# Down products ahead of the transposes, quarters first in up, and other places for scatters and gathers, in the expert stage of a two-layer trunk

## The chip, the cores and the metric

The kernel runs on one core of a Trainium2 chip. The metric is device time in microseconds. Before the change the median of three runs is 1512.02 us (1510.33 to 1512.49).

## The reference

Two layers over 256 tokens of 1024 columns, in float32. Layer 0 mixes tokens (RWKV-7 heads and forgetting attention) and ends in a dense SwiGLU. Layer 1 is a Conformer convolution and then a mixture of experts, which is what the change touches:

```python
def swiglu(x, w_gate, w_up, w_down):
    return (jax.nn.silu(x @ w_gate) * (x @ w_up)) @ w_down

logits = (xt @ w_router).astype(jnp.float32)
top_v, top_i = lax.top_k(logits, TOP_K)            # 2 of 8 experts for each of 256 tokens
top_w = jax.nn.softmax(top_v, axis=-1)
gates = jnp.sum(jax.nn.one_hot(top_i, N_EXPERTS) * top_w[..., None], axis=1)
for e in range(N_EXPERTS):                         # w_gate, w_up: 1024 x 3584, w_down: 3584 x 1024
    y = y + gates[:, e:e + 1] * swiglu(xt, w_gate[e], w_up[e], w_down[e])
```

A token belongs to two experts, so an expert needs only its own rows, 64 on average. All weights of all experts are read all the same.

## The kernel before

The stages follow each other: the mix of layer 0, its dense network, the convolution, and from about 575 us on the experts.

**Order of the experts.** A router counts and sorts the experts by their number of tokens. Seven are done one after the other, called experts 0 to 6 here in the order of their turn (`turn`, the index `n` in the code). The eighth, the one with the most tokens ("the largest", `big`), has no turn of its own: its work is cut into 21 phases, and `extra` says behind which chunk of which expert a phase stands (one in expert 1, six in 2, four in 3, three in 4, one in 5, six in 6).

**Chunks.** The hidden width 3584 is cut into 7 chunks of 512. A chunk of an expert is: gate (`project`, "g"), SiLU on ACT, up (`project`, "u"), `hidden`: DVE multiplies SiLU(gate) by up (L1311), TensorE transposes the product in blocks of 128 columns (L1314), ACT copies the transposes to SBUF (L1316). The down product (`down`) of a chunk runs one chunk later, on the copy that ACT made then.

**Arms.** How many rows an expert has sets its arm, chosen when the kernel runs. In the executions here experts 0, 3 and 4 run HALF (64 rows), experts 1 and 5 MOST (96 rows), experts 2 and 6 FEW (32 rows). With 64 rows the array is split into two halves of 64 columns (L1246 for gate and up, L1331 for down), each with its own part of the output. With 32 rows it is split into four quarters (L1252, L1337). MOST does both: 64 rows in halves and then 32 in quarters. A float32 product is two passes of the array and stands as two rows in the trace. Transposes, gathers and scatters use all 128 columns.

**The largest.** Its weights are split into a high and a low part, by ACT (L197) and then DVE (L198), and each product is three passes (L1274 for gate and up, L1293 to L1295 for down). `parts` has two buffers of each half, so the splits run at most two pieces ahead of TensorE.

**Gathers and scatters.** Before an expert begins, `gather` collects its rows by products with a one-hot matrix (L1168) and transposes that matrix (L1177). After it ends, `scatter` brings its output back to the tokens (L1196), and DVE adds it up (L1197). `hooks` says behind which chunk of an expert each of them stands.

**Weights.** Each chunk of a matrix is two loads of 1 MB, issued by SP (L1230) into a ring of 12 buffers. A load can be issued when TensorE (or the split) has read what the buffer held before.

**What sets the order.** The code is written for a scheduler that moves instructions within an engine's queue where it expects a wait. So the order on an engine is near that of the code, but not the same. In what follows it is read from the built programs.

Of the kernel before, what the change touches and what calls it, by code (L numbers as in the profile page):

```python
# [27 lines left out]
FULL, MOST, HALF, FEW = "full", "most", "half", "few"  # L28
# [84 lines left out]
class Trunk:  # L113
# [1121 lines left out]
    def project(self, ex, kind, c, mode, load):  # L1235
        nc, x = self.nc, ex["x"][0]
        p = self.mpsum("gu", "gu")
        ws = [load(ex, kind, c, i) for i in range(2)]
        ks = [(ws[kk // 4][:, kk % 4], kk, kk == 0, kk == NK - 1) for kk in range(NK)]
        if mode == FULL:  # L1240
            for w, kk, st, sp in ks:
                nc.tensor.matmul(p, x[:, kk], w, start=st, stop=sp)
        if mode in (MOST, HALF):
            for w, kk, st, sp in ks:
                for h in range(2):
                    nc.tensor.matmul(p[64 * h : 64 * h + 64, :T], x[:, kk, 0:64], w[:, T * h : T * h + T],  # L1246
                                     start=st, stop=sp, tile_position=(0, 64 * h), skip_group_check=True)
        if mode in (MOST, FEW):
            o, r = (T, 64) if mode == MOST else (0, 0)
            for w, kk, st, sp in ks:  # L1250
                for q in range(4):
                    nc.tensor.matmul(p[32 * q : 32 * q + 32, o : o + P], x[:, kk, r : r + 32], w[:, P * q : P * q + P],  # L1252
                                     start=st and o == 0, stop=sp, tile_position=(0, 32 * q), skip_group_check=True)
        return p


# [83 lines left out]
    def moe(self):  # L1340
        nc, tc, a = self.nc, self.tc, self.a
        nch = NCH
# [18 lines left out]
        def load(ex, *o):  # L1361
            w = early.get(o) if ex["n"] == 0 else None
            if w is None:
                w = self.egran(wt[wi[0] % nw], ex, *o)
            wi[0] += 1
            return w
# [18 lines left out]
        exs = []  # L1385
# [9 lines left out]
        def arm(n, mode, hooks, b=0, first=True, phases=True):  # L1395
            me = exs[n]
            if b:
                me = dict(me, x=me["x"][1:])
            if not first:
                me = dict(me, n=NE)  # L1400
            h = None
            for c in range(nch + 1):
                if c < nch:
                    s = self.silu(mode, self.project(me, "g", c, mode, load))
                    last, h = h, self.hidden(mode, s, self.project(me, "u", c, mode, load))
                else:
                    last = h
                if c == nch and phases:
                    phase(n, nch - 1)
                if c > 0:  # L1410
                    ws = [load(me, "d", c - 1, i) for i in range(2)]
                    self.down(mode, last, ws, yp, c == 1, c == nch)
                if c < nch - 1 and phases:
                    phase(n, c)
                if c in hooks:
                    hooks[c]()
            self.evac(mode, yp)

        def phase(n, c):
            if c not in extra.get(n, ()):  # L1420
                return
            k = sum(len(v) for j, v in extra.items() if j < n) + extra[n].index(c)
            cc, kind = k // 3, "gud"[k % 3]
            if kind == "d":
                self.big_down(big, cc, load, ysum)
                if cc == nch - 1:
                    for b in range(2):
                        self.evac(FULL, cols(ysum[b]))
                        self.scatter(big, b)
                return  # L1430
            ps = self.big_project(big, kind, cc, load)
            for j in range(2):
                js = slice(512 * j, 512 * j + 512)
                if kind == "g":
                    nc.scalar.activation(sb[j], ps[j], AF.Silu)
                else:
                    nc.vector.tensor_tensor(sb[j], sb[j], ps[j], op=ALU.mult)
                    self.split_psum(self.bh[0][:, js], self.bh[1][:, js], sb[j])
# [15 lines left out]
        yp = [self.mpsum("yp", "y") for _ in range(2)]  # L1454
        form = value(self.cnt0[0:1, 0:1], 2)
        extra = {1: (6,), 2: (0, 1, 2, 3, 4, 6), 3: (0, 2, 4, 6), 4: (1, 3, 5), 5: (6,), 6: (0, 1, 2, 3, 4, 5)}

        def hooks(n, first, last, prev):
            h = {}
            if prev is not None:  # L1460
                h[0] = prev
            if n == 0 and first:
                h[1] = ranks
                h[2] = lambda: self.gather(big, 0)
                h[3] = lambda: self.gather(big, 1)
            if last and n < len(exs) - 1:
                h[4] = lambda: self.gather(exs[n + 1], 0)
            elif last:
                h[2] = last_rows
            return h  # L1470
# [9 lines left out]
        for s, (members, arms) in enumerate(sets):  # L1480
            w0 = wi[0]

            def go(j):
                wi[0] = w0
                for n, modes in zip(members, arms[j]):
                    prev = (lambda n=n: self.scatter(exs[n - 1], 0)) if n > 0 else None
                    if len(modes) == 2:
                        if prev is not None:
                            prev()
                        self.gather(exs[n], 1)  # L1490
                        arm(n, modes[1], hooks(n, True, False, None), 1, True, False)
                        prev = lambda n=n: self.scatter(exs[n], 1)
                    first = len(modes) == 1
                    arm(n, modes[0], hooks(n, first, True, prev), 0, first)
# [11 lines left out]
            if s + 1 < len(sets):  # L1506
                sp = [mybir.EngineType.SP]
# [120 lines left out]
```

## Time and profile before

| | |
|---|---|
| median of three runs | 1512.02 us |
| the profiled execution | 1509.74 us, its span 1508.0 us |
| TensorE busy | 1423.2 us (94% of the span) |
| VectorE, ScalarE busy | 576.1 us, 450.1 us |
| read from HBM | 422.81 MB, 281 GB/s over the span |
| most that a fortieth of the span moved | 420 GB/s |

The expert stage is some 900 us of the span. Matmuls are pipelined and their ends are modelled, so TensorE shows as busy nearly throughout it; what a piece of work costs there is read from the start of its first instruction to the start of the next piece's first, and not from its busy time.

### The profile page before, as it was taken

How to read it: one execution, taken by the hardware profiler on the slowest of the kernel's cores; microseconds unless marked ns; L12 is line 12 of the kernel's file. 1: busy time of each engine (PE TensorE's matmuls, PEld its weight loads, DVE VectorE, ACT ScalarE, POOL GpSimd, SP SyncE). 2: the span in 40 equal slices, each digit the busy share in tenths (PEclk: the TensorE clock that was granted, in tenths of full speed). 3: DMA queues.
4: the chain of work that ended last, by engine and by line, in shares of the span. 5: the costliest groups of instructions: out<-in, count | busy, mean ns of one | idle time of the engine just before them, and what ended most of it. 6: DMA issues, size and time to landing. Idle time of an engine off the chain costs nothing. (4 is left out here: it accounts for less than half of the span.)

```text
span 1508.0 us, 32342 instructions
## 1 busy us (share of the span) xinstructions
PE 1423.2 (94%) x14162; PEld 1054.7 (70%) x14162; DVE 576.1 (38%) x980; ACT 450.1 (30%) x747; POOL 37.7 (3%) x63
## 2 busy tenths in 40 slices
PE   7999999999979998999999999999999999999995
PEld 6867768999966676656556787766666755657882
DVE  3855457555587663101002433321221210023435
ACT  5433435444456742110002232211211100013231
POOL 1100010000001100000000000000000000000000
PEclk8999999999989999999999999999999999999998
DMA  7322045555642238989988999899999999898992
GB/s 257 113 86 86 29 167 164 178 191 191 178 106 85 85 130 337 418 337 418 407 308 306 406 418 411 341 420 420 419 420 419 392 377 353 304 343 339 416 417 116
DMA packets 107208, 426.23 MB, mean 283 GB/s; under 512 B 6842, under 2 KB 55994, under 8 KB 64032
## 3 DMA queue, kind: packets, MB, share of 16 engines
q1 hardware_dynamic: 105968, 420.15, 72.3%
q0 software_dynamic: 1072, 3.74, 0.7%
q8 instruction: 118, 1.93, 0.5%
q14 instruction: 50, 0.41, 0.1%
HBM read 422.81 MB, written 1.05 MB: 281 GB/s over the span
## 5 line engine op out<-in xcount | busy, mean ns | idle before, releaser
L172 DVE TENSOR_TENSOR wl<-w,wh 128x1024 fp32r<-128x1024 f32 x122 | 150.8, 1239 | 120.5 <-ACT wh L170 120.1
L170 ACT ACTIVATE wh<-w 128x1024 fp32r<-128x1024 f32 x122 | 128.7, 1058 | 155.4 <-PE gu L209 56.4
L1311 DVE TENSOR_TENSOR sl<-sl,gu 128x256 f32<-128x256 f32 (+2 forms) x49 | 20.6, 421 | 400.6 <-PE gu L1252 244.1
L1274 PE MATMUL gu<-xl,bl 128*128 128x256 f32 x448 | 125.8, 286 | 3.4 <-DVE bl L198 3.2
L1246 PE MATMUL gu<-wr,xh 128*64 128x256 f32 x1024 | 122.2, 384 | 4.0 <-ACT yh L197 2.6
L1274 PE MATMUL gu<-xl,bh 128*128 128x256 f32 x448 | 125.6, 282 | 0.0
L1274 PE MATMUL gu<-xbl,bh 128*128 128x256 f32 x448 | 125.5, 281 | 0.0
L1246 PEld LDWEIGHTS gu<-wr,xh 128*64 128x64 f32 x1024 | 77.4, 138 | 43.9 <-issue 9.2
L208 PE MATMUL gu<-xh,wh 128*128 128x256 f32 x352 | 99.9, 286 | 2.4 <-DVE nt L825 2.4
L209 PE MATMUL gu<-xl,wh 128*128 128x256 f32 x352 | 100.2, 285 | 0.0
L210 PE MATMUL gu<-xh,wl 128*128 128x256 f32 x352 | 99.8, 284 | 0.0
L1305 ACT ACTIVATE sl<-gu 128x256 f32<-128x256 f32 (+2 forms) x49 | 18.8, 384 | 252.0 <-PE gu L1252 154.3
L1246 PE MATMUL gu<-wt,xh 128*64 128x256 f32 x768 | 93.1, 383 | 0.0
L1274 PEld LDWEIGHTS gu<-xl,bh 128*128 128x128 f32 x448 | 84.6, 189 | 5.4 <-issue 5.3
L1274 PEld LDWEIGHTS gu<-xl,bl 128*128 128x128 f32 x448 | 83.3, 188 | 5.8 <-DVE bl L198 5.8
L1274 PEld LDWEIGHTS gu<-xbl,bh 128*128 128x128 f32 x448 | 84.5, 189 | 0.1
L1331 PE MATMUL yp<-wr,ht 128*64 128x512 f32 x304 | 83.1, 600 | 0.0
L1316 ACT ACTIVATE ht<-ht 128x256 f32<-128x256 f32 (+2 forms) x49 | 18.8, 384 | 206.7 <-PE ht L1314 206.6
L1246 PEld LDWEIGHTS gu<-wt,xh 128*64 128x64 f32 x768 | 55.6, 137 | 31.2 <-issue 7.1
L198 DVE TENSOR_TENSOR bl<-wr,bh 128x1024 fp32r<-128x1024 f32 x40 | 48.1, 1224 | 56.5 <-ACT bh L197 56.5
L208 PEld LDWEIGHTS gu<-xh,wh 128*128 128x128 f32 x352 | 67.3, 192 | 3.4 <-DVE nt L825 2.0
L209 PEld LDWEIGHTS gu<-xl,wh 128*128 128x128 f32 x352 | 67.7, 192 | 0.7 <-DVE xl L826 0.3
(438 smaller groups left out, 2688.5 us busy)
## 6 DMA issues: line engine op xcount, KB each, us to landing
wr<-in_wd_dram SPq DMA_DIRECT2D x58, 1024.0 KB, 12.1
wr<-in_wg_dram SPq DMA_DIRECT2D x56, 1024.0 KB, 12.9
wr<-in_wu_dram SPq DMA_DIRECT2D x52, 1024.0 KB, 13.1
wt<-in_wg_dram SPq DMA_DIRECT2D x44, 1024.0 KB, 12.0
wt<-in_wd_dram SPq DMA_DIRECT2D x40, 1024.0 KB, 13.1
wx<-in_wu_dram SPq DMA_DIRECT2D x32, 1024.0 KB, 12.2
wt<-in_wu_dram SPq DMA_DIRECT2D x28, 1024.0 KB, 11.2
wx<-in_wd_dram SPq DMA_DIRECT2D x14, 1024.0 KB, 8.8
```

The source lines that it names most:

```text
L170: self.split_act = nc.scalar.activation(wh, w[:, k : k + g], AF.Copy)
L172: self.split_ins = nc.vector.tensor_tensor(wl, w[:, k : k + g], wh.bitcast(F32), op=ALU.subtract)
L198: nc.vector.tensor_tensor(lo, src, hi.bitcast(F32), op=ALU.subtract)
L208: nc.tensor.matmul(ps, wh[:, cols], xh[:, k], start=first and k == 0, stop=False, skip_group_check=True)
L209: nc.tensor.matmul(ps, wh[:, cols], xl[:, k], start=False, stop=False, skip_group_check=True)
L210: nc.tensor.matmul(ps, wl[:, cols], xh[:, k], start=False, stop=k == NK - 1, skip_group_check=True)
L1246: nc.tensor.matmul(p[64 * h : 64 * h + 64, :T], x[:, kk, 0:64], w[:, T * h : T * h + T], start=st, stop=sp, tile_position=(0, 64 * h), ski ...
L1274: mm = lambda l, r, st, sp: nc.tensor.matmul(o, l[:, k, cols], r[:, kk], start=st, stop=sp, skip_group_check=True)
L1305: self.nc.scalar.activation(s[:, :w], gate[:, :w], AF.Silu)
L1311: self.last_mul = nc.vector.tensor_tensor(s[:, :w], s[:, :w], up[:, :w], op=ALU.mult)
L1316: nc.scalar.activation(h[:, :w], ps[:, :w], AF.Copy)
L1331: nc.tensor.matmul(y[0][64 * d : 64 * d + 64], h[:, o : o + 64], w[:, 512 * d : 512 * d + 512], start=st, stop=sp, tile_position=(0, 64 * ...
```

## The change

Three edits. In `arm`, the down product of the chunk before is written between the up projection and `hidden` (multiply, transposes, copy), where it stood behind `hidden`. In `project`, the up projection of a MOST expert does its quarters first and its halves after them. In `hooks`, a scatter goes to the first chunk of its expert that has a phase, a gather to the first such chunk from the third on, and both stand ahead of the phase of their chunk, not behind it.

```diff
--- before.py
+++ after.py
@@ -1237,20 +1237,25 @@
         p = self.mpsum("gu", "gu")
         ws = [load(ex, kind, c, i) for i in range(2)]
         ks = [(ws[kk // 4][:, kk % 4], kk, kk == 0, kk == NK - 1) for kk in range(NK)]
-        if mode == FULL:
-            for w, kk, st, sp in ks:
-                nc.tensor.matmul(p, x[:, kk], w, start=st, stop=sp)
-        if mode in (MOST, HALF):
+        def wide():
             for w, kk, st, sp in ks:
                 for h in range(2):
                     nc.tensor.matmul(p[64 * h : 64 * h + 64, :T], x[:, kk, 0:64], w[:, T * h : T * h + T],
-                                     start=st, stop=sp, tile_position=(0, 64 * h), skip_group_check=True)
-        if mode in (MOST, FEW):
+                                     start=st and not up, stop=sp, tile_position=(0, 64 * h), skip_group_check=True)
+
+        def narrow():
             o, r = (T, 64) if mode == MOST else (0, 0)
             for w, kk, st, sp in ks:
                 for q in range(4):
                     nc.tensor.matmul(p[32 * q : 32 * q + 32, o : o + P], x[:, kk, r : r + 32], w[:, P * q : P * q + P],
-                                     start=st and o == 0, stop=sp, tile_position=(0, 32 * q), skip_group_check=True)
+                                     start=st and (up or o == 0), stop=sp, tile_position=(0, 32 * q), skip_group_check=True)
+
+        up = kind == "u" and mode == MOST
+        if mode == FULL:
+            for w, kk, st, sp in ks:
+                nc.tensor.matmul(p, x[:, kk], w, start=st, stop=sp)
+        for f in {MOST: (narrow, wide) if up else (wide, narrow), HALF: (wide,), FEW: (narrow,)}.get(mode, ()):
+            f()
         return p
 
 
@@ -1398,22 +1403,21 @@
                 me = dict(me, x=me["x"][1:])
             if not first:
                 me = dict(me, n=NE)
-            h = None
             for c in range(nch + 1):
                 if c < nch:
                     s = self.silu(mode, self.project(me, "g", c, mode, load))
-                    last, h = h, self.hidden(mode, s, self.project(me, "u", c, mode, load))
-                else:
-                    last = h
-                if c == nch and phases:
+                    up = self.project(me, "u", c, mode, load)
+                elif phases:
                     phase(n, nch - 1)
                 if c > 0:
                     ws = [load(me, "d", c - 1, i) for i in range(2)]
-                    self.down(mode, last, ws, yp, c == 1, c == nch)
+                    self.down(mode, h, ws, yp, c == 1, c == nch)
+                if c < nch:
+                    h = self.hidden(mode, s, up)
+                if c in hooks:
+                    hooks[c]()
                 if c < nch - 1 and phases:
                     phase(n, c)
-                if c in hooks:
-                    hooks[c]()
             self.evac(mode, yp)
 
         def phase(n, c):
@@ -1457,14 +1461,16 @@
 
         def hooks(n, first, last, prev):
             h = {}
+            ph = extra.get(n, ()) if last else ()
             if prev is not None:
-                h[0] = prev
+                h[next((c for c in ph if c < nch - 1), 0)] = prev
             if n == 0 and first:
                 h[1] = ranks
                 h[2] = lambda: self.gather(big, 0)
                 h[3] = lambda: self.gather(big, 1)
             if last and n < len(exs) - 1:
-                h[4] = lambda: self.gather(exs[n + 1], 0)
+                at = [c for c in ph if 3 <= c < nch - 1 and c not in h]
+                h[at[0] if at else 4] = lambda: self.gather(exs[n + 1], 0)
             elif last:
                 h[2] = last_rows
             return h
```

The first place is TensorE's queue in expert 1 (MOST), from the up projection of chunk 2 on: `gu` is the projection, `yp` the down product, `ht` the transposes, `wx` and `wt` are weights. Before:

```order
L1246 MATMUL gu_7752<-wx_5515,xh_5551 64x256 x8
L1246 MATMUL gu_7752<-wx_5516,xh_5551 64x256 x8
L1252 MATMUL gu_7752<-wx_5515,xh_5551 32x128 x16
L1252 MATMUL gu_7752<-wx_5516,xh_5551 32x128 x16
L1331 MATMUL yp_5673<-wt_5517,ht_7671 64x512
L1314 MATMUL ht_7804<-cstT,sl_7750 128x128 x3
L1331 MATMUL yp_5673<-wt_5517,ht_7671 64x512 x3
L1331 MATMUL yp_5673<-wt_5518,ht_7671 64x512 x4
L1337 MATMUL yp_5674<-wt_5517,ht_7671 32x256 x8
L1337 MATMUL yp_5674<-wt_5518,ht_7671 32x256 x8
```

The same place now:

```order
L1250 MATMUL gu_7699<-wr_5530,xh_5551 32x128 x16
L1250 MATMUL gu_7699<-wr_5531,xh_5551 32x128 x16
L1250 MATMUL gu_7752<-wx_5515,xh_5551 32x128 x16
L1250 MATMUL gu_7752<-wx_5516,xh_5551 32x128 x16
L1243 MATMUL gu_7752<-wx_5515,xh_5551 64x256 x8
L1243 MATMUL gu_7752<-wx_5516,xh_5551 64x256 x8
L1336 MATMUL yp_5673<-wt_5517,ht_7697 64x512 x4
L1336 MATMUL yp_5673<-wt_5518,ht_7697 64x512 x4
L1342 MATMUL yp_5674<-wt_5517,ht_7697 32x256 x8
L1342 MATMUL yp_5674<-wt_5518,ht_7697 32x256 x8
L1319 MATMUL ht_7830<-cstT,sl_7750 128x128 x3
L1243 MATMUL gu_7836<-wt_5519,xh_5551 64x256 x8
```

The quarters of up now follow those of gate, the halves of up are followed by the halves of down, and the transposes have left the middle of the down product for its end. The chunks of expert 5 read alike, and chunks 3 and 4 of both before had a second break, with one product of the quarters between two halves of the down product.

The second place is TensorE's queue in expert 0 (HALF), the end of chunk 2, where a gather follows (`ga`, `ot`). Before:

```order
L1331 MATMUL yp_5673<-wt_5517,ht_5772 64x512
L1314 MATMUL ht_5870<-cstT,sl_5848 128x128 x2
L1331 MATMUL yp_5673<-wt_5517,ht_5772 64x512 x3
L1331 MATMUL yp_5673<-wt_5518,ht_5772 64x512 x4
L1168 MATMUL ga_5888<-oh_5885,tok_5277 128x128 x8
L1168 MATMUL ga_5899<-oh_5885,tok_5277 128x128 x8
L1177 MATMUL ot_5910<-cstT,oh_5885 128x128 x2
```

The same place now:

```order
L1336 MATMUL yp_5673<-wt_5517,ht_5780 64x512 x4
L1336 MATMUL yp_5673<-wt_5518,ht_5780 64x512 x4
L1319 MATMUL ht_5880<-cstT,sl_5848 128x128 x2
L1168 MATMUL ga_5888<-oh_5885,tok_5277 128x128 x8
L1168 MATMUL ga_5899<-oh_5885,tok_5277 128x128 x8
L1177 MATMUL ot_5910<-cstT,oh_5885 128x128 x2
```

The transposes stand behind the whole down product and ahead of the gather. In experts 0, 3 and 4 ten down products lose their break in this way: chunks 1 to 5 of expert 0 (in chunk 5 the transposes go to the middle, between two even halves), 1, 3 and 5 of expert 3, and 2 and 4 of expert 4 (chunk 6 of it too, where the down product that follows waits for the copy). Where a phase of the largest follows, the transposes stood ahead of the down product as a whole, and still do, in most places.

The third place is TensorE's queue in expert 4 (HALF), from the transposes ahead of the scatter (`sca`) of expert 3. Before, behind chunk 0:

```order
L1314 MATMUL ht_14158<-cstT,sl_14136 128x128 x2
L1196 MATMUL sca_14163<-yh,oht_5641 128x512
L1196 MATMUL sca_14163<-yl,oht_5641 128x512
L1246 MATMUL gu_14179<-wt_5517,xh_5551 64x256
L1196 MATMUL sca_14167<-yh,oht_5641 128x512
L1196 MATMUL sca_14167<-yl,oht_5641 128x512
L1246 MATMUL gu_14179<-wt_5517,xh_5551 64x256 x2
L1196 MATMUL sca_14171<-yh,oht_5641 128x512
L1196 MATMUL sca_14171<-yl,oht_5641 128x512
L1246 MATMUL gu_14179<-wt_5517,xh_5551 64x256
L1196 MATMUL sca_14175<-yh,oht_5641 128x512
L1196 MATMUL sca_14175<-yl,oht_5641 128x512
```

Now, behind chunk 1:

```order
L1319 MATMUL ht_14214<-cstT,sl_14182 128x128 x2
L1196 MATMUL sca_14219<-yh,oht_5641 128x512
L1196 MATMUL sca_14219<-yl,oht_5641 128x512
L1196 MATMUL sca_14223<-yh,oht_5641 128x512
L1336 MATMUL yp_5673<-wr_5526,ht_14161 64x512 x4
L1196 MATMUL sca_14223<-yl,oht_5641 128x512
L1196 MATMUL sca_14227<-yh,oht_5641 128x512
L1196 MATMUL sca_14227<-yl,oht_5641 128x512
L1196 MATMUL sca_14231<-yh,oht_5641 128x512
L1336 MATMUL yp_5673<-wr_5527,ht_14161 64x512 x4
L1196 MATMUL sca_14231<-yl,oht_5641 128x512
L1298 MATMUL y_14237<-bh_14239,bhh 128x512
```

The scatter was spread among the gate's halves of chunk 1, and now stands among the down product of chunk 0, directly ahead of a phase of the largest (`y`). The gather of expert 4 has moved in the same way, from behind chunk 4, which has no phase, to chunk 3, ahead of a phase. In expert 2 the gather has moved from the phase of chunk 4 to that of chunk 3. The other scatters stood ahead of the phase before, and stand there now. The order of the loads on SP is unchanged within an expert.

## Rows read from the trace of the kernel before

**Rows 1.** Windows of experts 0, 1, 3, 5: us, busy by engine, PEclk, DMA share, GB/s.

```profile
582.30:675.50 93.20, 91.94 (x677) 55.68 (x676) 13.43 (x54) 12.73 (x27) 0.00 (x0) 1.00 0.91 368
678.60:802.80 124.20, 124.12 (x1651) 74.34 (x1653) 8.55 (x17) 7.37 (x16) 0.00 (x0) 0.99 0.95 378
...
952.40:1071.50 119.10, 115.09 (x824) 79.70 (x824) 27.55 (x38) 20.95 (x32) 0.00 (x0) 0.99 1.01 415
...
1215.30:1339.60 124.30, 123.18 (x1653) 73.56 (x1655) 8.75 (x15) 8.32 (x17) 0.00 (x0) 1.00 0.89 340
```

**Rows 2.** Waits of PE in the expert stage: total us, times, longest us.

```profile
PE ht L1314 <- DVE sl L1311: 12.8, 23, 0.8
...
PE gu L1274 <- DVE bl L198: 3.2, 4, 1.2
```

**Rows 3.** Waits of ACT in the same stretch.

```profile
ACT bh L197 <- DMA wt<-in_wd_dram: 2.6, 2, 1.4
```

**Rows 4.** Timeline of PE, chunk 2 of expert 1 (start us, us, engine, line, tiles).

```profile
713.20 3.67 PE L1246 MATMUL gu<-wr,xh 128*64 128x256 f32 x32
716.80 1.95 PE L1252 MATMUL gu<-wr,xh 128*32 128x128 f32 x64
718.69 3.67 PE L1246 MATMUL gu<-wx,xh 128*64 128x256 f32 x32
...
724.18 1.07 PE L1331 MATMUL yp<-wt,ht 128*64 128x512 f32 x2
725.18 0.55 PE L1314 MATMUL ht<-cstT,sl 128*128 128x128 f32 x3
725.66 3.65 PE L1331 MATMUL yp<-wt,ht 128*64 128x512 f32 x14
729.24 1.93 PE L1337 MATMUL yp<-wt,ht 128*32 128x256 f32 x32
731.10 0.44 PE L1246 MATMUL gu<-wt,xh 128*64 128x256 f32 x2
```

**Rows 5.** Timeline of PE, end of chunk 3 of expert 1.

```profile
749.69 0.65 PE L1246 MATMUL gu<-wr,xh 128*64 128x256 f32 x4
```

**Rows 6.** Timeline of PE, chunk 3 of expert 0, up to its gather.

```profile
636.64 3.62 PE L1246 MATMUL gu<-wx,xh 128*64 128x256 f32 x32
640.09 1.02 PE L1331 MATMUL yp<-wt,ht 128*64 128x512 f32 x2
641.04 0.44 PE L1314 MATMUL ht<-cstT,sl 128*128 128x128 f32 x2
641.41 3.65 PE L1331 MATMUL yp<-wt,ht 128*64 128x512 f32 x14
644.99 0.38 PE L1168 MATMUL ga<-oh,tok 128*128 128x128 f32 x1
```

**Rows 7.** Timeline of PE, a down product of expert 3 in one piece.

```profile
1071.52 3.65 PE L1331 MATMUL yp<-wt,ht 128*64 128x512 f32 x16
1075.11 0.39 PE L1274 MATMUL gu<-xl,bh 128*128 128x256 f32 x1
```

**Rows 8.** Timeline of PE, quarters of expert 2.

```profile
929.79 1.93 PE L1252 MATMUL gu<-wt,xh 128*32 128x128 f32 x64
931.53 1.93 PE L1252 MATMUL gu<-wr,xh 128*32 128x128 f32 x64
```

**Rows 9.** Timeline of PE, chunks 1 and 2 of expert 3.

```profile
983.36 1.02 PE L1331 MATMUL yp<-wr,ht 128*64 128x512 f32 x2
...
995.82 0.44 PE L1314 MATMUL ht<-cstT,sl 128*128 128x128 f32 x2 [0.58 <-DVE sl L1311]
```

**Rows 10.** Timeline of PE behind a gather: expert 2 into a phase of the largest.

```profile
911.41 0.74 PE L1293 MATMUL y<-bh,bhh 128*128 128x512 f32 x2 [1.42 <-ACT bh L197]
912.67 0.50 PE L1294 MATMUL y<-bl,bhh 128*128 128x512 f32 x1 [0.52 <-DVE bl L198]
```

**Rows 11.** Timeline of PE behind the gather of expert 3.

```profile
1040.63 0.39 PE L1274 MATMUL gu<-xl,bl 128*128 128x256 f32 x1 [1.22 <-DVE bl L198]
```

## The prediction

> **What bounds the kernel now.** I read the windows first, one per expert. They show TensorE busy almost from end to end in each, and the DMA engines full or nearly so: share 0.91 for expert 0, 0.95 for expert 1, 1.01 for expert 3, 0.89 for expert 5 [rows 1]. Either could be the bound, so the waits decide. In the whole expert stage TensorE's longest list entry is the transposes waiting for DVE's multiply, 12.8 us in 23 waits, then the split of a weight, 3.2 us [rows 2]; no wait of TensorE for a load is among them. A load shows as the end of a wait in one place, at ACT's split, 2.6 us in two waits [rows 3]. So the stage runs at TensorE's pace, with the weights a little ahead, and the rest of the kernel before it isn't touched.
>
> Next I read TensorE's timeline, from start to start. A MOST chunk lasts from 713.20 to 731.10, 17.90 us. In it the down product in halves is torn: two passes take 1.00 us (724.18 to 725.18), the three transposes 0.48, the other fourteen 3.58 [rows 4]. The same sixteen passes in one piece take 3.59 us with the step to the next shape, 1071.52 to 1075.11 [rows 7]. So the tear costs about 1.0 us beside the transposes. Two reasons fit: the passes of the two halves run side by side in pairs, and a break after an odd product leaves a pass of each without its partner at both ends (0.50 us a pass ahead of the break, 0.22 in one piece); and TensorE stands until DVE's multiply is done.
>
> **The change part by part.** Work is neither added nor removed on any engine; it moves.
>
> *Prices.* Halves of gate, then quarters: 3.60 us; quarters, then halves: 1.89 [rows 4]. Quarters followed by quarters: 1.74 (929.79 to 931.53) [rows 8], so a change of shape costs 0.15. Halves of up followed by halves of down: 3.45 (636.64 to 640.09) [rows 6]. Quarters of down, then another shape: 1.86. Transposes: 0.48 for three [rows 4] and 0.37 for two [rows 6], each with the step to the halves, so 0.11 each and 0.15 for the step.
>
> *A MOST chunk.* New order: 3.60 + 1.74 + 1.89 + 3.45 + 3.59 + 1.86 + 0.48 = 16.61 us, 1.29 less than 17.90. The multiply on DVE now has the whole down product, 5.4 us, to be done in. Chunk 3 lasted 731.10 to 749.69, 18.59 us [rows 4, 5], as a second break by a product in quarters cost 0.69 more, and chunk 4 is ordered alike: 1.98 each. In chunks 4 and 6 a gather or a phase follows the transposes at full width, so one step of 0.15 goes too. In chunk 0 there's no down product, only two changes of shape less: 0.29. One MOST expert saves 0.29 + 3 x 1.29 + 2 x 1.98 + 1.29 + 2 x 0.15 = 9.7 us; experts 1 and 5 together 19.4. The last step, transposes behind quarters, stands nowhere in the trace of before: at best it's free, at worst it drains like the halves of 64 columns, 0.95 - 0.43 = 0.5 us [rows 6]; I take the 0.15 of the other steps.
>
> *A HALF chunk.* Before a gather: 0.95 + 0.37 + 3.58 = 4.90 us from 640.09 to 644.99 [rows 6]. Now 3.59 + two transposes 0.22 = 3.81, and the gather follows in the same shape: 1.09 saved, three times in expert 0. Without a gather the next chunk's halves fill the lone passes up, so less is to be had: from 983.36 to the end of the second up, 995.82 - 0.58, are 11.9 us [rows 9], and now 3.59 + 0.37 + 2 x 3.45 + 0.2 = 11.1: 0.8 saved, in two chunks of expert 0, three of expert 3 and one of expert 4. In chunk 4 of expert 4 4.90 become 3.96, 0.9 saved. The last chunk of expert 4 gains its break back and loses about as much waiting for ACT's copy: nothing. Sum 3.3 + 6 x 0.8 + 0.9 = 9.0 us.
>
> *Hooks ahead of a phase.* The products are the same. What changes is what stands behind them in the queues of ACT and DVE: the split of the phase's weights waits until the copies of the gather or the sums of the scatter are done. The price stands in the trace where a gather is ahead of a phase already: 1.42 + 0.52 us in expert 2 [rows 10], 1.22 in expert 3 [rows 11]. New are the gather and the scatter of expert 4: 2 x 1.22 = 2.4 us. In expert 2 the stall moves with the gather from one phase to another; the phase it leaves then has only 1.86 us of quarters as cover, where copy and split take longer, and one phase there has later transposes: 0.7 in all. Bounds for these four: nothing, if the scheduler's order hides them, to twice the price, 6 us. I take 3.1. On SP the load of the last norm's rows goes four loads earlier; the weights ahead in the ring hide it.
>
> *The stream.* Expert 3 asks for 50 loads in its turn (42 of its own, 8 for four phases); at 415 GB/s a load of 1.05 MB takes 2.53 us, so 126 us, more than the 119.10 that its window has [rows 1]. It lives on what the ring holds, and ACT's two waits for loads lie there and near the end [rows 3]. What is saved ahead of such a wait is given back: I take off one HALF chunk, 0.8. Experts 1 and 5 ask for 44 loads, 111 us; they'd last 124.2 - 9.7 = 114.5. That still fits.
>
> Sum: 19.4 + 9.0 - 3.1 - 0.8 = 24.5 us off the profiled execution's 1509.74: 1485.2. The median of the runs shown is 2.3 us above that execution, so 1487.5.
>
> **The Trainium skill on the tear.** The rows show 4.90 us for a torn down product with its transposes, and by the rows of one in one piece 3.81 to 3.96 [rows 6, 7]. "TensorEngine Tiling (Array Packing)", section "Key Properties", says that a change of the tiling mode drains TensorE, while tiles run on their own; by that alone, only the number of changes counts. That is the first rival below.
>
> **Rivals.**
>
> 1. *Only the changes of shape count.* The lone passes aren't why the torn product is slow, the modelled starts only look so. Then a MOST chunk saves three changes of 0.15, 0.45 us, chunks 3 and 4 0.69 more, chunk 0 0.29; a HALF chunk 0.15 to 0.3. That is 2 x (0.29 + 6 x 0.45 + 2 x 0.69) = 8.7, plus 2.2, less 3.1: 7.8 us, 1504. For it: the busy times of these rows are modelled. Against: a pass takes 0.50 us ahead of the break and 0.22 in one piece, on starts alone [rows 4, 7]. Chance 0.07.
>
> 2. *The stream takes it back.* Wherever the DMA share is 0.94 and more, a faster TensorE waits for weights, and only experts 0 and 5 keep what they save: 3.3 + 1.6 + 9.7 = 14.6, with the stalls of the hooks hidden in the same waits: 1497. For it: shares of 0.95 and 1.01 [rows 1]. Against: TensorE's list has no wait for a load [rows 2], and 44 loads fit in 114 us. Chance 0.12. [...]
>
> 3. *Slower: the splits of the phases come late.* ACT and DVE work in order, and the copy of the transposes stands ahead of the split. If the transposes are last ahead of a phase, copy and split have no cover any more and the stall of 1.94 us [rows 10] is paid at each of 21 phases: 41 us, less 24.5 + 3.1 saved: 13 us slower, 1525. It decides from 14 such phases on. Against: in the built order the transposes stay ahead of the down product at most phases, and in expert 1 two splits stand ahead of the copy. Chance 0.03.
>
> 4. *More than forecast.* Nothing is lost at the hooks and the transposes' last step is free: 24.5 + 3.1 + 12 x 0.15 = 29, 1483. Chance 0.08, and within the range.
>
> **How the numbers follow.** The forecast has 0.70, 1482 to 1494 for it alone. The range, 1481 to 1502, adds rivals 2 and 4 and leaves out most of 1 and 3. About 0.2%, 3 us, is what a measurement of this kernel tells from no change. Rivals 1, 2 and 4 and the forecast are all faster by more: 0.93, taking 0.04 off for a mix of 1 and 2 with dear stalls, which ends within 0.2%. Slower: 0.03.
>
> **What would show it.** In the profile after: MOST chunks of 16.6 us from gate to gate; sixteen passes of L1336 without a break, 3.4 to 3.6 us; transposes behind the quarters of down with no wait for DVE, whose 12.8 us shrink to the places ahead of phases; the gathers of expert 0 directly behind the transposes; a wait of 1 to 2 us for a split behind the gather and the scatter of expert 4. Wrong would be: TensorE waits for loads in experts 1 or 5 (rival 2), MOST chunks of 17.4 us (rival 1), or waits for splits at most phases (rival 3).

## The result, and the profile after

The changed kernel took 1493.15 us (median of four runs, 1492.38 to 1499.99) against 1511.17 us of the kernel before (four runs, 1509.52 to 1512.49): a ratio of 0.9874, 95% interval 0.9847 to 0.9901. Five more runs, later, gave 1492.96 us and 0.986, 0.9839 to 0.988. The forecast was 1487.5 within 1481 to 1502, faster: right in sign and range, and 5.7 us too far down. Of the 24.5 us that the sum had taken off, 18.0 came in the medians, and 16.3 in the span of the profiled executions (1508.0 to 1491.7).

First the windows of the changed kernel, one each for experts 1, 3 and 5 (us; busy us of TensorE, its weight loads, VectorE, ScalarE and GpSimd; TensorE's granted clock; DMA share; GB/s; to be held against [rows 1]).

```profile
680.40:795.00 114.60, 113.62 (x1642) 72.29 (x1640) 9.80 (x16) 9.26 (x17) 0.00 (x0) 1.00 0.99 402
944.60:1063.60 119.00, 113.97 (x838) 77.09 (x840) 28.79 (x39) 23.26 (x35) 0.00 (x0) 1.00 1.01 416
1208.00:1322.00 114.00, 112.55 (x1646) 73.22 (x1644) 7.02 (x11) 8.31 (x16) 0.00 (x0) 1.00 0.93 357
```

The same work of a MOST expert now lasts some 114 us and not 124, and the DMA share rose with it, from 0.95 to 0.99 in expert 1. A share of 0.99 still isn't a wait: these are TensorE's longest waits in the changed kernel's expert stage (us in total, times, longest).

```profile
PE ht L1319 <- DVE sl L1316: 12.0, 21, 0.8
PE gu L1243 <- issue: 6.9, 4, 3.2
PE gu L1279 <- DVE bl L198: 6.0, 6, 1.2
...
PE y L1299 <- DVE bl L198: 2.4, 3, 1.5
```

No wait of TensorE's products for a load is in that list, short ones included, which disposes of rival 2. Its weight loads did wait for DMA, 0.3 us at a time and 2.1 us in all in experts 1 and 5, but beside running products: every chunk there with no gather or phase near takes the same 16.61 us. The first row has hardly moved from 12.8 us in 23 waits [rows 2]; the other three stand for what the change cost. Waits for the split were 3.2 us [rows 2] and 0.8 us before, and the waits with no releaser ("issue") were these:

```profile
PE gu L1246 <- issue: 4.3, 2, 2.8
```

Now TensorE's timeline of chunk 2 of expert 1, start to start, as in [rows 4].

```profile
711.35 3.67 PE L1243 MATMUL gu<-wr,xh 128*64 128x256 f32 x32
714.95 1.95 PE L1250 MATMUL gu<-wr,xh 128*32 128x128 f32 x64
716.72 1.93 PE L1250 MATMUL gu<-wx,xh 128*32 128x128 f32 x64
718.58 3.67 PE L1243 MATMUL gu<-wx,xh 128*64 128x256 f32 x32
722.09 3.60 PE L1336 MATMUL yp<-wt,ht 128*64 128x512 f32 x16
725.62 1.93 PE L1342 MATMUL yp<-wt,ht 128*32 128x256 f32 x32
727.48 0.55 PE L1319 MATMUL ht<-cstT,sl 128*128 128x128 f32 x3
727.96 3.67 PE L1243 MATMUL gu<-wt,xh 128*64 128x256 f32 x32
```

From 711.35 to 727.96 are 16.61 us, the forecast to the second decimal, and each step within 0.06 of its term: 3.60, 1.77, 1.86, 3.51, 3.53, 1.86, 0.48. Sixteen passes of L1336 run without a break, and the transposes follow the quarters without a wait. In chunk 3 of expert 0 the gather follows the transposes directly (TensorE again, against [rows 6]):

```profile
641.86 3.60 PE L1336 MATMUL yp<-wt,ht 128*64 128x512 f32 x16
645.39 0.44 PE L1319 MATMUL ht<-cstT,sl 128*128 128x128 f32 x2
645.66 3.74 PE L1168 MATMUL ga<-oh,tok 128*128 128x128 f32 x32
```

3.80 us stand where 4.90 stood; the forecast was 3.81.

**Where the time went, term by term.** The length of each chunk is the distance between two starts of ACT's silu. It repeats to 0.05 us from one profile to the next of the same code, but for the chunks behind a branch and those in which TensorE's clock fell.

| part | forecast, us saved | in the profiles |
|---|---|---|
| chunks 1 to 6 of experts 1 and 5 | 18.8 | 9.50 + 9.37 = 18.9 |
| chunk 0 of experts 1 and 5 | 0.6 | -0.39 - 0.47 = -0.9 |
| HALF chunks of experts 0, 3, 4 | 9.0 | 4.85 + 2.50 + 0.81 + 1.19 = 9.35 |
| last chunk of expert 4 | 0 | -1.4 |
| scatter and gather of expert 4 | -2.4 | -1.56 - 1.85 = -3.4 |
| expert 2 | -0.7 | -1.7 |
| stream | -0.8 | 0 |
| rest of the stage (behind branches) | 0 | 0.7 in chunk 6 of expert 0, -0.7 elsewhere: 0 |
| ahead of the expert stage | 0 | -4.6 |

The gather's 1.85 and the last 1.19 of the HALF chunks fall in the same two chunks and are told apart by after_old_hooks, below. The sum of the stage is 20.8 us for 24.5 forecast; the stage began 4.6 us later than before, at 590.67 us and not 586.10, though no edit touches what is ahead of it.

### The profile page after: what moved, and what is told of

Its sections match the earlier page's. It is cut to its first block, busy times and chain, and to the rows that moved or that the text cites. A ratio compares the mean times of both kernels' runs of the same rounds, so it can differ in the third digit from the quotient of the medians.

```text
span 1491.7 us, 32344 instructions
## 1 busy us (share of the span) xinstructions
PE 1399.1 (94%) x14162; PEld 1050.8 (70%) x14162; DVE 575.2 (39%) x980; ACT 450.8 (30%) x747; POOL 37.8 (3%) x63
## 5 line engine op out<-in xcount | busy, mean ns | idle before, releaser
L1243 PE MATMUL gu<-wr,xh 128*64 128x256 f32 x1024 | 116.9, 381 | 6.2 <-issue 3.2
L1243 PEld LDWEIGHTS gu<-wr,xh 128*64 128x64 f32 x1024 | 72.9, 137 | 45.0 <-issue 8.3
L1321 ACT ACTIVATE ht<-ht 128x256 f32<-128x256 f32 (+2 forms) x49 | 18.8, 384 | 282.4 <-PE ht L1319 282.4
L1310 ACT ACTIVATE sl<-gu 128x256 f32<-128x256 f32 (+2 forms) x49 | 18.8, 385 | 185.9 <-PE gu L1250 110.5
L1336 PE MATMUL yp<-wr,ht 128*64 128x512 f32 x304 | 69.8, 595 | 0.5 <-ACT ht L1321 0.5
L210 PEld LDWEIGHTS gu<-xh,wl 128*128 128x128 f32 x352 | 67.0, 190 | 0.6 <-DVE wl L172 0.6
```

Source lines behind the costliest of these rows:

```text
L210: nc.tensor.matmul(ps, wl[:, cols], xh[:, k], start=False, stop=k == NK - 1, skip_group_check=True)
L1336: nc.tensor.matmul(y[0][64 * d : 64 * d + 64], h[:, o : o + 64], w[:, 512 * d : 512 * d + 512], start=st, stop=sp, tile_position=(0, 64 * ...
```

## Experiments

Eleven runs followed, eight of new kernels and three repeats. The first three do one edit of the three alone, the fourth undoes one. A MOST chunk is the best measure of all: eight times (chunks 1, 2, 3 and 5 of experts 1 and 5) it repeats with no gather, scatter or phase near. In the table, which shows expert 1, T is the transposes and the numbers are passes of the halves:

| kernel | chunk 1 | 2 | 3 | order of the down product |
|---|---|---|---|---|
| before | 17.90 | 17.90 | 18.59 | 2 passes, T, 14; in chunk 3 a stray quarter too |
| arm_only | 16.90 | 17.60 | 17.60 | 16, quarters, T; in 2 and 3 a stray quarter |
| quarters_only | 17.61 | 17.61 | 17.61 | 2, T, 14 |
| break_odd | 17.61 | 17.61 | 17.61 | 10, T, 6, then the quarters |
| break_even | 16.77 | 16.76 | 16.76 | 12, T, 4, then the quarters |
| changed | 16.61 | 16.61 | 16.61 | 16, quarters, T |

### One edit alone: down ahead of the transposes

```diff
-                    last, h = h, self.hidden(mode, s, self.project(me, "u", c, mode, load))
+                    up = self.project(me, "u", c, mode, load)
...
+                if c < nch:
+                    h = self.hidden(mode, s, up)
```

> The kernel before with one edit of the three: the down products are written ahead of the transposes; quarters stay last in up, gathers and scatters stay behind the phases. Theory A (a break inside the sixteen passes of L1331 leaves two passes without their partner, and the wait for the gating product is paid in the open): a MOST chunk goes from 17.90 us to about 16.9, and from 18.59 to 16.9 in chunks 3 and 4, HALF chunks as in the changed kernel (0.8 to 1.1 less each); about 15 us in the MOST experts, 8 to 9 in the HALF ones, less about 1.4 where the code of expert 5 is fetched after a shorter tail: 1488 to 1490. Rival B (only the changes of tile shape count; a break costs two of them, 0.3 us): a MOST chunk about 17.6, 1504 to 1506. Rival C (the gain of the whole change came from quarters first): no change, 1509 to 1512.

Measured: 1490.66 us in the profiled execution, two of four runs at 1490.5 and two at 1501.6, so a median of 1496.06; ratio 0.9898, 0.985 to 0.9945. The two pairs differ in the mean granted clock, 0.980 and 0.972; the kernel is the same. The stage took 902.7 us for 921.9. Chunk 1 came as theory A has it, 16.90, and so did the HALF chunks. Chunks 2 to 4 missed it by 0.70: this is TensorE in chunk 2.

```profile
717.27 1.94 PE L1331 MATMUL yp<-wt,ht 128*64 128x512 f32 x8
719.14 0.62 PE L1337 MATMUL yp<-wt,ht 128*32 128x256 f32 x2
719.69 1.94 PE L1331 MATMUL yp<-wt,ht 128*64 128x512 f32 x8
721.56 1.93 PE L1337 MATMUL yp<-wt,ht 128*32 128x256 f32 x30
```

The scheduler draws one quarter product, two passes, in between the halves. They take 0.55 us for 0.12 among their like, and two more changes of shape come with them. The same stray made chunk 3 of the kernel before 18.59 us long. With quarters first in up it is gone. Chunk 1 puts rivals B and C out.

### One edit alone: quarters first

```diff
-                                     start=st, stop=sp, tile_position=(0, 64 * h), skip_group_check=True)
+                                     start=st and not up, stop=sp, tile_position=(0, 64 * h), skip_group_check=True)
...
+        for f in {MOST: (narrow, wide) if up else (wide, narrow), HALF: (wide,), FEW: (narrow,)}.get(mode, ()):
```

> The kernel before with one edit of the three: in up, the quarters are written ahead of the wide products. The order dw, T, dw with its broken pair stays. Theory A: 0.29 us less in each of 14 MOST chunks (two changes of tile shape fewer), less 0.7 us in the first chunk of experts 1 and 5, where the many short instructions come before the fetch of code has caught up: 2 to 3.5 us less, 1507.5 to 1509.5. Rival C (it carries the gain): 1500 or less. Rival D (the stalls of the fetch cost more than the shapes give): 1511 to 1514.

Measured: 1507.0 us (ten runs), ratio 0.9961, 0.9943 to 0.998; the stage 916.7 us, 5.2 less. More than expected, for a reason I hadn't put down: chunks 1, 2 and 5 save their 0.29, but chunks 3 and 4 save 0.98, as the stray quarter goes with the new order. Chunk 0 saved 0.31 in expert 1 and lost 1.52 in expert 5. In chunk 2 of expert 1 the transposes stand behind the first product, as in the kernel before, and wait for nothing:

```profile
726.66 1.02 PE L1336 MATMUL yp<-wt,ht 128*64 128x512 f32 x2
727.61 0.55 PE L1319 MATMUL ht<-cstT,sl 128*128 128x128 f32 x3
728.09 3.65 PE L1336 MATMUL yp<-wt,ht 128*64 128x512 f32 x14
```

### One edit alone, and one undone: gathers and scatters

```diff
+                if c in hooks:
+                    hooks[c]()
                 if c < nch - 1 and phases:
                     phase(n, c)
-                if c in hooks:
-                    hooks[c]()
...
-                h[0] = prev
+                h[next((c for c in ph if c < nch - 1), 0)] = prev
...
+                at = [c for c in ph if 3 <= c < nch - 1 and c not in h]
+                h[at[0] if at else 4] = lambda: self.gather(exs[n + 1], 0)
```

> The kernel before with one edit of the three: gathers and scatters ahead of a phase of the largest. Theory A (the product of the phase waits for the split on VectorE and ScalarE, which now has only a gather or a scatter as cover, whose matmuls wait in turn; 1.5 us each at expert 4's scatter, expert 4's gather, expert 2's gather): 4 to 5 us longer, 1515 to 1517. The prediction's own term: 3.1 us longer, 1514. Rival E (those stalls are there whichever side the gather stands, and the changed kernel's gaps are of its shorter chunks): within 1 us of before, 1510 to 1512.

> The changed kernel with that third edit undone: gathers and scatters behind the phase, at the old chunks. Theory A: 4 to 5 us shorter than the changed kernel, 1488 to 1489.5, the gain at the chunks 1 and 2 (scatter) and 4 and 5 (gather) of expert 4 and 4 and 5 of expert 2. The prediction's term: 3.1 shorter, 1490. Rival E: as the changed kernel, 1492.5 to 1494.

Measured: hooks_only 1518.44 us (ten runs), ratio 1.0033, 1.0013 to 1.0054, the stage 926.9 us, 5.0 more than before. after_old_hooks 1487.13 us (four runs), ratio to the kernel before 0.9823, 0.9795 to 0.9852, the stage 897.2 us, 3.9 less than in the changed kernel's first profile and 2.6 less than in its shortest. So this edit slows the kernel, alone and in company; rival E is out. Chunks 0 and 1 of expert 4, which hold the scatter, by ACT's silu at the start of chunk 0 and of chunk 2, in the changed kernel:

```profile
1083.18 0.39 ACT L1310 ACTIVATE sl<-gu 128x256 f32<-128x256 f32 x1 [1.52 <-PE gu L1243]
1119.24 0.39 ACT L1310 ACTIVATE sl<-gu 128x256 f32<-128x256 f32 x1 [8.16 <-PE gu L1243]
```

and in after_old_hooks:

```profile
1080.30 0.38 ACT L1310 ACTIVATE sl<-gu 128x256 f32<-128x256 f32 x1 [1.52 <-PE gu L1243]
1114.79 0.38 ACT L1310 ACTIVATE sl<-gu 128x256 f32<-128x256 f32 x1 [8.15 <-PE gu L1243]
```

36.06 us for 34.49: the scatter costs 1.57 where it now stands. TensorE of the changed kernel shows what is late, once behind the scatter and once behind the gather (two rows, far apart):

```profile
1104.58 0.51 PE L1299 MATMUL y<-bl,bhh 128*128 128x512 f32 x1 [1.52 <-DVE bl L198]
...
1144.15 0.39 PE L1279 MATMUL gu<-xl,bl 128*128 128x256 f32 x1 [1.22 <-DVE bl L198]
```

Both wait for DVE's half of the split, as forecast; 1.52 and 1.22 us for 1.22 twice. Chunks 3 and 4 of expert 4, with the gather, lose 1.85 us against after_old_hooks.

Expert 2 didn't go as theory A has it. Its chunks 3 and 4 took 42.49 us before, 42.54 in hooks_only, 44.00 in the changed kernel, and 43.98 in after_old_hooks, which has the gather where it was. The 1.5 us is not the move's. It isn't chance either: the three profiles of the changed kernel have 43.99 to 44.05, and arm_only, best_try and tail_even8, with the gather in its old place, 43.94 to 44.07. Windows of the changed kernel around that gather (columns as above):

```profile
881.00:885.40 4.40, 2.46 (x17) 2.02 (x18) 2.63 (x3) 2.28 (x3) 0.00 (x0) 1.00 1.01 413
885.40:888.80 3.40, 3.40 (x18) 3.40 (x17) 0.42 (x1) 0.09 (x1) 0.00 (x0) 0.50 1.02 422
```

and of the same stretch in break_odd (below), which has the same order and the same two waits there:

```profile
887.80:892.20 4.40, 2.46 (x17) 2.02 (x18) 2.61 (x3) 2.27 (x3) 0.00 (x0) 1.00 1.01 415
892.20:895.60 3.40, 3.40 (x31) 3.40 (x31) 0.83 (x2) 1.06 (x1) 0.00 (x0) 1.00 1.02 422
```

TensorE was busy 2.46 of 4.40 us while it waited for the split, and then got the lower of its two clocks, 0.50 (1.2 GHz), for 3.4 us. In after_old_hooks the same befell it behind its gather, at 900.0 us. In break_odd TensorE was busy for the same 2.46 of 4.40 us, the clock stayed at 1.00, and the two chunks took 42.52 us. So a wait in this place can cost itself and 1.5 us more; why the clock falls in the one kernel and not in the other stays open.

### Why a torn down product is slow

The break of the kernel before could cost a lone pass at either side, a wait for DVE's multiply, or only the two changes of shape. These two kernels put the transposes inside the down product again, but late enough that the multiply is done.

```diff
                 for d in range(2):
+                    if mid and 2 * kb + d == 5:
+                        mid()
                     nc.tensor.matmul(y[0][64 * d : 64 * d + 64], h[:, o : o + 64], w[:, 512 * d : 512 * d + 512],
...
+                    mid = (lambda: new.append(self.hidden(mode, s, up))) if mode == MOST and c < nch else None
...
```

In break_even the 5 is a 6.

> The changed kernel, but in MOST arms the transposes are written inside the sixteen wide down passes, behind the fifth of the eight products (ten passes; 2.2 us, more than the wait for the gating product). In nothing else does it differ from break_even, where they stand behind the sixth. Theory A (the passes run in pairs, one to a column half; a break behind an odd number leaves one pass without its partner on either side, 0.85 us in all): a MOST chunk 16.61 + 0.85 + up to 0.3 for the second change of shape = 17.5 to 17.8 in all twelve chunks 1 to 6, some 10 us longer than break_even. Theory B (only the change of shape costs, or the open wait): both kernels alike, 16.6 to 16.9.

> As break_odd with the transposes behind the sixth product. Theory A: 16.6 to 16.9 in a MOST chunk (no pass loses its partner; one pair of shape changes more than the changed kernel), and the whole within 4 us of the changed kernel. Theory B: as break_odd.

Measured: break_odd 1504.93 us (three runs), ratio 0.9944, 0.9924 to 0.9964. break_even 1498.42 us (two runs, 1495.14 and 1501.71; the profiled one entered the stage 6 us later than break_odd's), ratio 0.9902, 0.9871 to 0.9934. Free of that, the stage took 912.2 and 902.1 us: 10.0 longer for the odd one, as theory A has it. TensorE in chunk 2 of expert 1, break_odd:

```profile
723.54 2.74 PE L1338 MATMUL yp<-wt,ht 128*64 128x512 f32 x10
726.21 0.55 PE L1319 MATMUL ht<-cstT,sl 128*128 128x128 f32 x3
726.69 1.93 PE L1338 MATMUL yp<-wt,ht 128*64 128x512 f32 x6
728.55 1.93 PE L1344 MATMUL yp<-wt,ht 128*32 128x256 f32 x32
```

and break_even:

```profile
729.14 2.75 PE L1338 MATMUL yp<-wt,ht 128*64 128x512 f32 x12
731.82 0.55 PE L1319 MATMUL ht<-cstT,sl 128*128 128x128 f32 x3
732.29 1.08 PE L1338 MATMUL yp<-wt,ht 128*64 128x512 f32 x4
733.30 1.93 PE L1344 MATMUL yp<-wt,ht 128*32 128x256 f32 x32
```

Ten passes take as long as twelve (2.67 and 2.68 us), and six take 1.86 us where four take 1.01. No wait stands at either. Halves and transposes are 5.01 us with the odd break and 4.16 with the even one, 0.85 us for the lone passes alone. By theory B they'd be equal. Two further breaks agree: a break behind two passes and one behind ten both give 17.61 us (quarters_only, break_odd), and in best_try, below, four passes ahead of an even break take 0.96 us, where two ahead of an odd one take 0.95 [rows 6].

### Repairs, and the tail of expert 4

```diff
-        up = kind == "u" and mode == MOST
+        up = kind == "u" and mode == MOST and c > 0
...
+                    mid = (lambda: new.append(self.hidden(mode, s, up))) if n == 4 and c == nch - 1 else None
```

with the old hooks of after_old_hooks, and `mid` called behind the second down product (best_try) or the fourth (tail_even8).

> The changed kernel with the hooks of before (as after_old_hooks), and two small repairs: in the last chunk of expert 4, which no phase follows, the transposes stand behind the second of the down products, so that TensorE's last wait comes 6 us ahead of the branch and not 3.5; and the first chunk of an expert has its quarters last again. Theory A (the code behind the branch is fetched once that last wait is over, some 7 to 8.5 us): chunk 6 of expert 4 about 20 us for 23.15, or for 21.6 where no half clock fell into it; first chunks of experts 1 and 5 as before (14.9) for 15.3 and 14.7: 1484 to 1486. Rival (the gap at the branch has its fixed length behind the last product): 1486.5 to 1488, chunk 6 of expert 4 at 21.5 or more.

> As best_try, but in the last chunk of expert 4 the transposes stand behind the fourth of the down products and not the second. Twenty-four passes of 0.22 us are left behind them in place of 28. If the code behind the branch comes 6.9 us after the hidden copy is there (the changed kernel's distance): first product behind the branch 12.9 us after the chunk's start, gap 2.1. If it comes as in best_try 9.1 us behind the transposes: 14.2 us, gap 3.4. If TensorE's instructions ahead of the branch are a queue of fixed length: gap 2.5 again, first product at 13.3. The whole within 1 us of best_try, 1482.5 to 1484.5.

Measured: best_try 1483.53 us (six runs), ratio to the kernel before 0.9816, 0.9789 to 0.9843; tail_even8 1484.34 us (four), 0.9827, 0.9799 to 0.9854. Their stages, 894.9 and 895.1 us, are 5 to 6 us shorter than the changed kernel's and the shortest measured. Chunk 0 of experts 1 and 5 took 15.12 and 14.88 us with quarters last, against 15.28 to 15.62 in three profiles of the changed kernel; over all kernels with quarters first it lay anywhere from 14.58 to 16.40. At the end of expert 4 and the start of expert 5, TensorE of the changed kernel:

```profile
1199.84 0.44 PE L1319 MATMUL ht<-cstT,sl 128*128 128x128 f32 x2
1200.75 3.65 PE L1336 MATMUL yp<-wr,ht 128*64 128x512 f32 x16 [0.47 <-ACT ht L1321]
1207.64 3.67 PE L1243 MATMUL gu<-wr,xh 128*64 128x256 f32 x32 [3.23 <-issue]
...
1212.79 1.62 PE L1250 MATMUL gu<-wr,xh 128*32 128x128 f32 x51 [0.92 <-issue]
...
1217.89 2.59 PE L1243 MATMUL gu<-wx,xh 128*64 128x256 f32 x22 [0.41 <-issue]
```

The kernel before, in the same place:

```profile
1206.86 7.08 PE L1331 MATMUL yp<-wr,ht 128*64 128x512 f32 x30
1215.38 0.87 PE L1246 MATMUL gu<-wr,xh 128*64 128x256 f32 x6 [1.44 <-issue]
...
1220.65 1.73 PE L1252 MATMUL gu<-wr,xh 128*32 128x128 f32 x53 [1.04 <-issue]
```

And best_try:

```profile
1188.43 0.44 PE L1319 MATMUL ht<-cstT,sl 128*128 128x128 f32 x2
1188.80 6.23 PE L1340 MATMUL yp<-wr,ht 128*64 128x512 f32 x28
1197.55 5.36 PE L1243 MATMUL gu<-wr,xh 128*64 128x256 f32 x32 [2.53 <-issue]
```

"issue" is time in which TensorE waited for nothing that the trace shows. Behind the branch into expert 5 it grew from 1.44 to 3.23 us. The stop in the gate's quarters, ahead of chunk 0's first silu, was there before too (1.04 us, now 0.92). What is new lies in chunk 0 itself: behind two runs of quarters TensorE stops once more, 0.41 us, in the halves of up. With quarters last no profile has that stop. Theory A said that 6.9 us pass from the last wait's end (1200.75 to 1207.64); then best_try, with 28 passes behind its last transposes, would have had a gap of 1.2 us. It had 2.53, so the theory is wrong in that form. tail_even8, with 24 passes, had 2.40: the distance of 6.9 us asks for 2.1, a queue of fixed length ahead of the branch for 2.5. That speaks for the queue, but 0.3 us and two kernels don't settle it, and the kernel before, 1.44 with 30 passes at a slower pace, wasn't resolved further. best_try still gained 2.5 us in this chunk over after_old_hooks (20.69 for 23.15): 0.5 at the transposes, 0.75 at the gap, and the rest because less of the low clock fell behind the branch, which isn't shown to be the repair's work. Against the changed kernel's three profiles (21.46 to 21.73) it gained 0.8 to 1.0 us.

### The changed kernel and the kernel before, once more

Unaltered, for the 4.6 us ahead of the stage.

> The changed kernel unaltered, for how long it takes up to the expert stage, whose code no edit touches: 590.67 us in its first profile, 586.06 to 589.22 in the five others. If that was chance of the clock in that execution: 586 to 590 now, the expert stage at 901 again, the whole 1488 to 1494. If it belongs to this kernel: 590.5 to 591.

> The changed kernel unaltered, a third profile. Its first two entered the expert stage at 590.67 and 590.96 us, seven profiles of kernels with the same code up to there at 586.06 to 597.74. If that is chance of the clock in an execution, anything from 586 to 598, with half-clock time ahead of the stage to match (34 us of it at 586, 51 at 590.8, 61 at 597.7); if it belongs to the kernel, 590.5 to 591 a third time.

> The kernel before unaltered, a second profile. If chance: the stage starts anywhere from 586 to 598 (586.10 in its first). If it belongs to the kernel: 586.0 to 586.3. Either way the chunks of the stage repeat to 0.05 us but for those behind a branch and those with a half clock in them (chunk 6 of experts 0 and 4, chunk 0 of 1, 2, 3 and 5).

Measured: after_again 1492.96 us, its stage from 590.96; after_third 1492.35 us, from 590.82; before_second 1510.42 us, from 586.76. Windows from the span's start to the stage, of the changed kernel and of the kernel before:

```profile
0.00:590.60 590.60, 551.56 (x4794) 455.08 (x4796) 350.73 (x645) 281.96 (x481) 37.83 (x63) 0.96 0.43 140
```

```profile
0.00:586.10 586.10, 547.01 (x4796) 453.31 (x4798) 351.15 (x645) 281.58 (x481) 37.70 (x63) 0.97 0.44 141
```

Same instructions, same work of DVE, another mean clock. Three profiles of the changed kernel lie within 0.3 us, so by what was written beforehand the delay would belong to it; the first profiles of the others lay anywhere from 586.06 to 597.74. But other numbers on record speak against that. The runs of this kernel go from 1489.62 to 1499.99 us, at clocks of 0.979 and 0.971, and a stage that repeats to 1.3 us can't hold that spread; so the time ahead of it most likely varies from run to run. All three profiles have a low clock of 17 us near the start (from 18.4 to 35.5 us in the first), where both profiles of the kernel before have it only 3.4 to 6.8 us at a time; but break_even, with the same code up to there, has the 17 us too. So the delay is one of the granted clock, and whether it belongs to the kernel stays open.

## Why the prediction was right, and where it was off

- *MOST chunks* (19.4 us): right, and for the first of the two reasons it gave. break_odd against break_even shows the lone passes by themselves, 0.85 us; break_even against the changed kernel shows one change of shape more, 0.16; quarters_only shows the two others, 0.29. Together they make up the 1.29. The second reason, the wait for DVE's multiply, falls: the transposes in [rows 4] have no wait beside them, break_odd with the multiply long done takes 17.61 us, and quarters_only with the transposes right behind the first product takes the same. TensorE's list of the kernel before has no such wait in experts 1 and 5; its 12.8 us lay in the other five experts, ahead of phases above all, where the order stayed. I read a total over the stage as if it stood in the chunk of the argument, and so forecast that it would shrink; it is 12.0.
- *Rival 1* (only shape changes): a change of shape does cost, 0.15 us as the rows gave it, but break_odd and break_even have the same changes and differ by 0.85 us in each chunk. The Trainium skill, "TensorEngine Tiling (Array Packing)", section "Key Properties", says that a change of the tiling mode drains TensorE. The trace agrees in that each change costs, and shows that it isn't all.
- *Rivals 3 and 4*: rival 3 needed late splits at most of 21 phases; TensorE has eleven waits for a split, for seven before. Rival 4 needed nothing lost at the hooks; they lost 3.4 us.
- *Chunk 0* (0.6 us): the wrong sign, -0.9. The step "only two changes of shape less" overlooked that quarters are 64 short instructions, and that with two runs of them behind a branch TensorE stops in the halves of up, 0.38 to 0.68 us in experts 1 and 5 of all three profiles. Where quarters are first and no such stop shows (expert 1 of quarters_only, expert 5 of break_even, break_odd and after_old_hooks), the chunk took 14.58 to 14.81 us, at best the 0.3 less that was forecast. That it runs out of instructions there is argued from this and not shown. With quarters last again best_try has 14.88 to 15.12.
- *HALF chunks* (9.0 us): right, 9.35 came. The term "loses about as much waiting for ACT's copy: nothing" for the last chunk of expert 4 failed: 0.47 us of that wait and 1.8 us more at the branch, less some 0.9 that the lone passes and a shorter stop in the quarters gave back: -1.4.
- *Hooks* (-3.1 us): the mechanism right in expert 4 and its size too small, 3.4 for 2.4 us. The two waits shown are 2.7 of it, and the scatter's own wait for DVE's sum is 0.4; the rest isn't resolved. In expert 2 the 0.7 for the moved stall was nothing (0.05 in hooks_only), and 1.5 us of low clock came in its place, in all three profiles.
- *The stream* (-0.8 us): nothing. Every HALF chunk of expert 3 kept its 0.83 us at a DMA share of 1.01. Rival 2's sign was products waiting for loads in experts 1 or 5, and there are none.
- *Ahead of the stage*: 4.6 us that no term held. It is the largest single piece of the 8.2 us between the forecast and the profiled execution.

## What to carry to other kernels

Where products run in pairs on parts of the array, count an interruption by the parity of what stands ahead of it: an even break costs its change of shape (0.16 us here), an odd one 0.85 us more, and a stray product of another shape 0.7. Before you credit a change with a wait that it covers, look for that wait in the very stretch, and not in a total over the stage. And measure an edit in three parts apart: here one of them cost 3 to 4 us of what the other two had won, and undoing it with two repairs gave 1483.5 us, the best of all kernels run.

## What the runs showed of the hardware

- Ten passes of 64 columns take 2.67 us, twelve 2.68, and six behind the break 1.86 us where four take 1.01: the two passes of a product without its partner cost about as much as the four of a pair.
- Behind the branch into expert 5 TensorE stood 1.4 to 3.3 us with no releaser in the trace. It often stood again in the first run of short instructions (1.04 us before, 0.92 in the changed kernel), and behind two such runs once more (0.41).
- A stretch in which TensorE was busy 2.46 of 4.40 us was followed by 3.4 us at the lower clock, 0.50; in another kernel with the same order, waits and busy time there, the clock stayed at 1.00.
- One kernel's executions lay 11 us apart (arm_only, 1490.5 and 1501.6) with a mean granted clock of 0.980 and 0.972. A gain of a few us is read from the stage's own length, which repeats to 1.3 us in the changed kernel's three profiles (901.1, 900.4, 899.7) and to 0.1 us in the two of the kernel before (921.9 both).
